# In the gate and up stage of a decoder layer, the product of block B21, which needs no sum, moves ahead to third place

## The chip, the cores and the metric

The kernel runs on one core of a Trainium2 chip. The metric is the device time of one execution in microseconds. The engines are TensorE (PE in the rows, PEld for its weight loads), VectorE (DVE), ScalarE (ACT), GpSimd (POOL, used here almost only to issue DMAs) and SyncE (SP, which issues the weight loads).

## What is computed

One layer of a hybrid decoder over 256 tokens of width 2048, in fp32: three attention branches, gated and merged, an output projection `w_out`, and then a SwiGLU sub-layer of inner width 5632. The change lies in the last of these:

```python
def swiglu(h, w_gate, w_up, w_down):
    return (jax.nn.silu(h @ w_gate) * (h @ w_up)) @ w_down
...
        h = rms_norm(x, norm_ffn_g[l])
        x = x + swiglu(h, w_ffn_gate[l], w_ffn_up[l], w_ffn_down[l])
    return rms_norm(x, final_norm_g)
```

## The kernel before, in words

**fp32 by two halves.** Each fp32 operand is split in two parts that TensorE can multiply: a rounded high part (ACT, line 806 for a gate or up weight) and the rest, the low part (DVE, line 811). A product is three matmuls for each 128 rows: high by high, low activation by high weight, high activation by low weight (`highs_first`, lines 783 to 794). With four slices of 128 rows a weight piece of 512 rows by 512 columns makes twelve matmuls of 128x512 for one PSUM bank.

**A gate and up pair.** `ffn_job(j)` (line 597), for j = 0 to 10, computes 512 columns of both gate and up for the 256 tokens. Of the four pieces of 512 rows, rows 0 and 1 go through a product of 2x2 blocks that has seven multiplications instead of eight (Strassen's scheme in Winograd's form); rows 2 and 3 are multiplied plainly. The blocks are B11 (up, rows 0), B12 (gate, rows 0), B21 (up, rows 1), B22 (gate, rows 1). An `m_unit` is one of the seven multiplications: twelve matmuls into one bank, with sums of activation blocks that were made once ("sp", `combine`, line 494). A `p_unit` is one plain piece for both token halves: twelve matmuls into each of two banks. Four banks are used under the names b6, b5, b8 and b1. The order before (lines 689 to 699) is

1. B11 into b6, copied out by ACT as m1 (`keep`, line 663)
2. B22 into b5
3. B11+B12 into b8, copied out as m5: the "first sum". DVE adds B12 into B11 ahead of its high part (line 612); behind its low part POOL issues a DMA that adds B22 from memory into the piece B12 (line 622, `accum_op`)
4. piece 2 of gate ("2,1") into b5, then b8
5. the "second sum", B11+B12+B22, into b6, copied out as u2, with another DVE add before and a DMA that adds B21 into B11 behind
6. piece 3 of gate ("3,1") into b5, then b8
7. the piece B12 with what was added, into b6, copied out as u3; after it `gate` on DVE and ACT
8. B21 into b1
9. piece 2 of up ("2,0") into b1, then b6
10. the piece B11 with all that was added, into b6
11. piece 3 of up ("3,0") into b1, then b6; after it `up` (lines 678 to 684), three DVE operations that free b6 and b1. 

Then f is transposed by TensorE, copied by ACT ("ft", line 577) and stored by a DMA, as side work of the next pair.

**Weight pieces** of 1 MB come by DMAs on SP's queue in the order of the loop at line 606. At most six raw pieces of this stage are live (`RAWS`, `pump`, line 764); each release of one lets in the next load. Raw pieces, high and low parts and two activation quads share 17 buffers of 1 MB.

**The order of issue** is fixed when the program is built, and each engine takes its instructions in that order. The main loop goes through the units:

```python
    for u, (need, later, stage, _, emit) in enumerate(units):
        prepare_units(u + 4 if stage == "mix" else u + 6)
        advance(1)
        todo, deferred[:] = deferred[:], []
        emit(ready.popleft())
        held -= need + later
        for f in todo:
            f()
```

`prepare_units` (line 934) works under a budget of nine parts for this stage. In steady state one step u issues: the add, if any, and the high part of unit u+4; the low part of unit u+3 with the release or the accumulating DMA behind it; one step of the side work (`advance`); the matmuls of unit u and its copy; then what was deferred. Where the stage begins, the step of the last `w_out` unit issues the low part of the first gate and up unit and the add and high part of the third; the step of the first unit issues the low parts of the second, third and fourth units and the high parts of the fourth and fifth.

**Side work at the start of the stage.** `evac_out(3)` (line 515) ends the mixer: DVE sums x2's last quarter (line 519), and its side steps follow in the first steps of the first pair: two empty ones, then eight transposes by TensorE with line 541 on ACT and line 542 on DVE for the four pieces of the quarter (in the step of the third unit), then ACT's row sums (line 485) and DVE's reciprocal root (in the step of the fourth).

Of the kernel before, what the change touches and what calls it, by code (L numbers as in the profile page):

```python
# [51 lines left out]
def trunk(ctx, tc, xT, x, gmix, gffn, w_in, b_gate, lq1, lk1, lq2, lk2, subln, w_branch, w_out,  # L52
# [12 lines left out]
    def slot(shape, name, dt=F32):  # L65
        return slots.tile(shape, dt, tag="slot", name=name)
# [92 lines left out]
    def quad(key):  # L159
        while key not in quads:  # L160
            assert side, key
            advance(1)
        return quads[key]
# [404 lines left out]
    def f_out(j, f):  # L568

        yield  # L570
        ps = [tps() for _ in range(2)]
        for t in range(2):
            transposes(ps[t], [f[:, t, i * P:(i + 1) * P] for i in range(4)])
        yield
        ft = slot([P, 4, S], "ft")
        for t in range(2):
            nc.scalar.activation(ft[:, :, t * P:(t + 1) * P], ps[t].rearrange("p (a b) -> p a b", a=4), AF.Copy)
        nc.gpsimd.dma_start(f_t[j], ft)
        yield
# [3 lines left out]
    def f_load(q):  # L583
        if q < NCF:
            f_in[q] = slot([P, 4, S], "fin")
            nc.gpsimd.dma_start(f_in[q], f_t[q])
# [10 lines left out]
    def ffn_job(j):  # L597

        B = {(k, n): (j, k, n) for k in range(4) for n in range(2)}
        B11, B12, B21, B22 = B[0, 0], B[0, 1], B[1, 0], B[1, 1]
        aps = {(j, k, n): (w_fu, w_fg)[n][j, k] for k in range(4) for n in range(2)}
        for key in (B11, B22, B12, B[2, 1], B[3, 1], B21, B[2, 0], B[3, 0]):
            want(key, aps[key], "ffn")
        bank = {}
        v = {}

        def add(dst, src):
            nc.vector.tensor_tensor(raw[dst], raw[dst], raw[src], OP.add)  # L612

        def m_unit(op, key, name, adds=(), drop=(), after=None, then=None):
            def prep():
                for d, s in adds:
                    add(d, s)
                h = high(raw[key])
                yield
                l = low(raw[key], h)  # L620
                if then:
                    nc.gpsimd.dma_start(raw[then[0]], aps[then[1]], accum_op=OP.add)
                release(*drop)
                yield h, l

            def emit(w):
                first = name not in bank
                if first:
                    bank[name] = accp.tile([P, 512], F32, tag="acc", name="acc")
                sh, sl = quad(("s", 0))[op]  # L630
                highs_first([(bank[name], sh, sl, first)], w)
                if after:
                    after()
            units.append((1, 1, "ffn", prep, emit))

        def p_unit(k, n, after=None):
            def prep():
                r = raw[B[k, n]]
                h = high(r)
                yield  # L640
                l = low(r, h)
                release(B[k, n])
                yield h, l

            def emit(w):
                qh, ql = quad(("h2", k))
                for t, name in enumerate((("b1", "b6"), ("b5", "b8"))[n]):
                    first = name not in bank
                    if first:
                        bank[name] = accp.tile([P, 512], F32, tag="acc", name="acc")  # L650
                    ts = slice(t * P, (t + 1) * P)
                    highs_first([(bank[name], qh[:, :, ts], ql[:, :, ts], first)], w)
                if after:
                    after()
            units.append((1, 1, "ffn", prep, emit))

        def keep(name, b):
            def f():
                if name == "m1":
                    v["m"] = slot([P, 2, 512], "m")  # L660
                    v["u"] = slot([P, 2, 512], "u")
                v[name] = v["m" if name[0] == "m" else "u"][:, int(name in ("m5", "u3"))]
                nc.scalar.activation(v[name], bank[b], AF.Copy)  # L663
                if name == "u2":
                    deferred.append(lambda: nc.vector.tensor_tensor(v["m5"], v["m5"], v["u2"], OP.subtract))
                if name == "u3":
                    deferred.append(gate)
            return f

        def gate():  # L670
            quad("rs2")
            s = v["s"] = slot([P, 2, 512], "sg")
            nc.vector.tensor_tensor(s[:, 0], bank["b5"], v["m5"], OP.add)
            nc.vector.tensor_tensor(s[:, 1], bank["b8"], v["u3"], OP.subtract)
            for t in range(2):
                nc.scalar.activation(s[:, t], s[:, t], AF.Silu, scale=rs2[:, t:t + 1])

        def up():

            s = v["s"]  # L680
            nc.vector.tensor_tensor(s[:, 1], bank["b6"], s[:, 1], OP.mult)
            nc.vector.tensor_tensor(v["m1"], bank["b1"], v["m1"], OP.add)
            nc.vector.tensor_tensor(s[:, 0], v["m1"], s[:, 0], OP.mult)
            side.append(f_out(j, s))

        def last():
            deferred.append(up)

        m_unit(0, B11, "b6", after=keep("m1", "b6"))
        m_unit(2, B22, "b5")  # L690
        m_unit(4, B11, "b8", adds=[(B11, B12)], after=keep("m5", "b8"), then=(B12, B22))
        p_unit(2, 1)
        m_unit(5, B11, "b6", adds=[(B11, B22)], drop=[B22], after=keep("u2", "b6"), then=(B11, B21))
        p_unit(3, 1)
        m_unit(6, B12, "b6", drop=[B12], after=keep("u3", "b6"))
        m_unit(1, B21, "b1", drop=[B21])
        p_unit(2, 0, after=(lambda: (f_load(0), f_load(1))) if j == NCF - 1 else None)
        m_unit(3, B11, "b6", drop=[B11])
        p_unit(3, 0, after=last)
# [61 lines left out]
    def want(key, ap, stage):  # L761
        wanted.append((key, ap, stage))
# [15 lines left out]
    def release(*keys):  # L778
        for k in keys:
            del raw[k]  # L780
        pump()

    def highs_first(todo, w):


        wh, wl = w
        for acc, ah, al, start in todo:
            for k in range(4):
                first = start and k == 0
                nc.tensor.matmul(acc, ah[:, k], wh[:, k], start=first, stop=False, skip_group_check=not start)  # L790
                nc.tensor.matmul(acc, al[:, k], wh[:, k], start=False, stop=False, skip_group_check=not start)  # L791
        for acc, ah, al, start in todo:
            for k in range(4):
                nc.tensor.matmul(acc, ah[:, k], wl[:, k], start=False, stop=k == 3, skip_group_check=not start)  # L794
# [9 lines left out]
    def high(r):  # L804
        h = big([P, 4, 512], "wh", F32R)
        nc.scalar.activation(h, r, AF.Copy)  # L806
        return h

    def low(r, h):
        l = big([P, 4, 512], "wl", F32R)  # L810
        nc.vector.tensor_tensor(l, r, h.bitcast(F32), OP.subtract)  # L811
        return l
# [72 lines left out]
    for j in range(NCF):  # L885
        ffn_job(j)
# [135 lines left out]
```

## Time and profile before

| | |
|---|---|
| median of 3 runs | 1666.36 us (1666.3 to 1666.77) |
| profiled execution | 1665.84 us, span 1663.7 us, mean granted clock 0.997 |
| PE, DVE, ACT busy in the span | 99%, 64%, 50% |
| chain that ended last | PE 97%, DVE 1%, DMA 1% |
| DMA | 352.65 MB moved, 212 GB/s in the mean |

The span runs from the first to the last instruction on the core. The share of an engine is its busy time over the span; matmuls overlap at their ends, so a busy PE is not one at its peak. The chain that ended last is followed back from the last instruction, at each step to what released it. Times in the rows are in microseconds from the span's start. In a timeline a bracket at the end of a row gives the idle time of the engine before it and what ended it.

### The profile page before, as it was taken

To read this page: it belongs to the slowest core of one execution; us is meant where nothing else is said; L and a number is where in the kernel's file an instruction comes from. 1 tells how busy PE (TensorE), PEld (TensorE's weight loads), DVE (VectorE), ACT (ScalarE), POOL (GpSimd) and SP (SyncE) were. 2 spreads that over 40 slices of the span, in tenths; PEclk is the share of its full clock that TensorE was granted. 3 is DMA by queue.
4 is the path that set the end of the run, shared out by engine and by line. 5 is a ranking of instruction groups with operands and counts; after the bars stand their busy time and mean duration, and the time that the engine had idled before them with its cause. 6 is when DMAs were issued, how large, how long until landed. Compare 5 with 4: busy or idle time off the path is not lost.

```text
span 1663.7 us, 18735 instructions
## 1 busy us (share of the span) xinstructions
PE 1645.7 (99%) x7512; PEld 1357.3 (82%) x7512; DVE 1065.9 (64%) x1077; ACT 824.1 (50%) x950; POOL 59.9 (4%) x87
## 2 busy tenths in 40 slices
PE   9999999999999999999999989999999999999997
PEld 6878788888888888888888878888888888888886
DVE  6675765555565556555565788777777776655463
ACT  7364554444444444444534465555555556444352
POOL 2100000000000000000000000000000001000000
PEclk9999999999999999999999999999999999999999
DMA  8544444444555555556675678888888888655561
GB/s 335 182 169 161 166 155 166 163 162 166 176 174 208 187 205 200 193 202 217 230 254 179 207 208 263 264 265 266 265 266 265 266 265 307 236 201 181 199 244 60
DMA packets 53656, 352.65 MB, mean 212 GB/s; under 512 B 6256, under 2 KB 6528, under 8 KB 13760
## 3 DMA queue, kind: packets, MB, share of 16 engines
q1 hardware_dynamic: 44640, 309.35, 51.4%
q0 software_dynamic: 8208, 41.04, 10.5%
q8 instruction: 59, 0.97, 0.2%
q10 hardware_dynamic: 720, 1.06, 0.2%
q14 instruction: 29, 0.24, 0.0%
HBM read 343.56 MB, written 7.86 MB: 211 GB/s over the span
## 4 chain that ended last, share of the span: by engine, by line
PE 97%; DVE 1%; DMA 1%; ACT 0%; issue 0%; SPq 0%; ACTq 0%; DVEq 0%
PE acc L800 22%; PE acc L802 22%; PE acc L801 22%; PE acc L790 9%; PE acc L791 9%; PE acc L794 9%; PE tps L206 2%; PE sps L245 1%; DVE wl L811 1%; DMA raw<-w_in_t 1%; PE sps L258 0%; PE sps L259 0%; PE sps L257 0%; PE sps L297 0%; PE sps L298 0%
## 5 line engine op out<-in xcount | busy, mean ns | idle before, releaser
L821 DVE TENSOR_TENSOR wboth<-raw,wboth 128x1024 fp32r<-128x1024 f32 (+1 forms) x410 | 500.7, 1235 | 316.3 <-ACT wboth L820 316.0
L820 ACT ACTIVATE wboth<-raw 128x1024 fp32r<-128x1024 f32 (+1 forms) x410 | 423.5, 1052 | 346.4 <-PE acc L802 284.5
L800 PE MATMUL acc<-wboth,hq 128*128 128x512 f32 x1472 | 586.3, 398 | 0.8 <-ACT wboth L820 0.8
L801 PE MATMUL acc<-wboth,hq 128*128 128x512 f32 x1472 | 573.4, 390 | 1.3 <-DVE wboth L821 1.3
L802 PE MATMUL acc<-wboth,hq 128*128 128x512 f32 x1472 | 574.4, 390 | 0.0
L811 DVE TENSOR_TENSOR wl<-raw,wh 128x2048 fp32r<-128x2048 f32 x121 | 275.9, 2289 | 81.2 <-PE acc L794 42.8
L802 PEld LDWEIGHTS acc<-wboth,hq 128*128 128x128 f32 x1472 | 276.3, 188 | 59.4
L800 PEld LDWEIGHTS acc<-wboth,hq 128*128 128x128 f32 x1472 | 276.5, 188 | 58.8 <-issue 2.7
L801 PEld LDWEIGHTS acc<-wboth,hq 128*128 128x128 f32 x1472 | 276.8, 188 | 57.6 <-DVE wboth L821 2.7
L806 ACT ACTIVATE wh<-raw 128x2048 fp32r<-128x2048 f32 x121 | 228.9, 1911 | 102.0 <-DVE raw L612 49.5
L790 PE MATMUL acc<-wh,hq 128*128 128x512 f32 x352 | 138.1, 392 | 5.2 <-ACT m L663 5.2
L791 PE MATMUL acc<-wh,hq 128*128 128x512 f32 x352 | 137.7, 391 | 0.0
L790 PE MATMUL acc<-wh,sp 128*128 128x512 f32 x308 | 120.8, 392 | 0.0
L791 PE MATMUL acc<-wh,sp 128*128 128x512 f32 x308 | 119.9, 389 | 0.0
L794 PE MATMUL acc<-wl,hq 128*128 128x512 f32 x352 | 94.1, 389 | 0.0
L790 PEld LDWEIGHTS acc<-wh,hq 128*128 128x128 f32 x352 | 66.6, 189 | 19.4 <-ACT m L663 5.6
L794 PE MATMUL acc<-wl,sp 128*128 128x512 f32 x308 | 82.4, 389 | 0.0
L791 PEld LDWEIGHTS acc<-wh,hq 128*128 128x128 f32 x352 | 66.7, 189 | 13.8
L794 PEld LDWEIGHTS acc<-wl,hq 128*128 128x128 f32 x352 | 66.1, 188 | 13.8
L794 PEld LDWEIGHTS acc<-wl,sp 128*128 128x128 f32 x308 | 57.8, 188 | 12.0
L791 PEld LDWEIGHTS acc<-wh,sp 128*128 128x128 f32 x308 | 57.9, 188 | 11.6
L790 PEld LDWEIGHTS acc<-wh,sp 128*128 128x128 f32 x308 | 57.9, 188 | 11.6
(193 smaller groups left out, 1044.5 us busy)
## 6 DMA issues: line engine op xcount, KB each, us to landing
raw<-w_in_t SPq DMA_DIRECT2D x116, 1024.0 KB, 4.9
raw<-w_fu_t SPq DMA_DIRECT2D x44, 1024.0 KB, 4.9
raw<-w_fg_t SPq DMA_DIRECT2D x44, 1024.0 KB, 6.6
raw<-w_fd_t SPq DMA_DIRECT2D x44, 1024.0 KB, 4.9
raw<-w_branch_t SPq DMA_DIRECT2D x24, 1024.0 KB, 4.9
raw<-w_out_t SPq DMA_DIRECT2D x16, 1024.0 KB, 4.9
raw<-w_fg_t POOLq DMA_DIRECT2D x11, 1024.0 KB, 7.9
raw<-w_fu_t POOLq DMA_DIRECT2D x11, 1024.0 KB, 8.8
```

Source lines behind the costliest of these rows:

```text
L206: nc.tensor.transpose(dst[:, i * P:(i + 1) * P], s, ident)
L245: nc.tensor.matmul(ps[:, a:b], qt[lo:hi, h, t * P:(t + 1) * P], kt[lo:hi, h, 0:b - a], start=True, stop=True)
L790: nc.tensor.matmul(acc, ah[:, k], wh[:, k], start=first, stop=False, skip_group_check=not start)
L791: nc.tensor.matmul(acc, al[:, k], wh[:, k], start=False, stop=False, skip_group_check=not start)
L794: nc.tensor.matmul(acc, ah[:, k], wl[:, k], start=False, stop=k == 3, skip_group_check=not start)
L800: nc.tensor.matmul(acc, ah[:, k], wh[:, k], start=start and k == 0, stop=False)
L801: nc.tensor.matmul(acc, ah[:, k], wl[:, k], start=False, stop=False)
L802: nc.tensor.matmul(acc, al[:, k], wh[:, k], start=False, stop=stop and k == n - 1)
L806: nc.scalar.activation(h, r, AF.Copy)
L811: nc.vector.tensor_tensor(l, r, h.bitcast(F32), OP.subtract)
L820: nc.scalar.activation(h[:, sl], r[:, sl], AF.Copy)
L821: nc.vector.tensor_tensor(l[:, sl], r[:, sl], h[:, sl].bitcast(F32), OP.subtract)
```

## The change

The unit of B21 becomes the third, behind that of B22 and ahead of the first sum, and the loads follow: B21's piece third, B12's fourth, then the rest in their order. The operations are the same in kind and number.

```diff
@@ -603,7 +603,7 @@
-        for key in (B11, B22, B12, B[2, 1], B[3, 1], B21, B[2, 0], B[3, 0]):
+        for key in (B11, B22, B21, B12, B[2, 1], B[3, 1], B[2, 0], B[3, 0]):
             want(key, aps[key], "ffn")
@@ -688,12 +688,12 @@
         m_unit(0, B11, "b6", after=keep("m1", "b6"))
         m_unit(2, B22, "b5")
+        m_unit(1, B21, "b1", drop=[B21])
         m_unit(4, B11, "b8", adds=[(B11, B12)], after=keep("m5", "b8"), then=(B12, B22))
         p_unit(2, 1)
         m_unit(5, B11, "b6", adds=[(B11, B22)], drop=[B22], after=keep("u2", "b6"), then=(B11, B21))
         p_unit(3, 1)
         m_unit(6, B12, "b6", drop=[B12], after=keep("u3", "b6"))
-        m_unit(1, B21, "b1", drop=[B21])
         p_unit(2, 0, after=(lambda: (f_load(0), f_load(1))) if j == NCF - 1 else None)
         m_unit(3, B11, "b6", drop=[B11])
         p_unit(3, 0, after=last)
```

## Rows read from the trace of the kernel before

**Rows 1.** The page's first part: busy time, share of the span, instructions of each engine.
```profile
PE 1645.7 (99%) x7512; PEld 1357.3 (82%) x7512; DVE 1065.9 (64%) x1077; ACT 824.1 (50%) x950; POOL 59.9 (4%) x87
```

**Rows 2.** Stretches: length, then busy time by engine, granted clock, DMA share, GB/s.
```profile
core 0: us, PE busy (x) PEld busy (x) DVE busy (x) ACT busy (x) POOL busy (x), PEclk, DMA share, GB/s
950.00:965.00 15.00, 9.83 (x49) 7.90 (x47) 13.88 (x11) 8.30 (x10) 0.88 (x1) 0.99 0.83 258
...
965.00:966.00 1.00, 1.00 (x3) 0.81 (x4) 1.00 (x1) 1.00 (x1) 0.00 (x0) 0.50 1.03 213
...
1045.70:1087.40 41.70, 41.70 (x190) 34.63 (x189) 33.23 (x20) 25.02 (x20) 2.31 (x4) 1.00 0.83 265
```

**Rows 3.** Waits from 936 to 985: us in total, times, the longest.
```profile
PE acc L790 <- ACT m L663: 5.2, 1, 5.2
```

**Rows 4.** TensorE's matmuls in order of time, 936 to 985: start, duration, what.
```profile
947.81 0.39 PE L790 MATMUL acc<-wh,sp 128*128 128x512 f32 x1
...
950.53 0.39 PE L790 MATMUL acc<-wh,sp 128*128 128x512 f32 x1
...
964.92 0.80 PE L790 MATMUL acc<-wh,hq 128*128 128x512 f32 x1 [5.17 <-ACT m L663]
...
969.21 0.39 PE L790 MATMUL acc<-wh,sp 128*128 128x512 f32 x1
```

**Rows 5.** ACT in order of time, 936 to 985.
```profile
963.91 0.47 ACT L541 ACTIVATE hq<-tps,gf 128x256 fp32r<-128x256 f32 x1 [0.58 <-DVE hq L542]
964.28 0.59 ACT L663 ACTIVATE m<-acc 128x512 f32<-128x512 f32 x1
964.76 1.91 ACT L806 ACTIVATE wh<-raw 128x2048 fp32r<-128x2048 f32 x1
966.56 0.60 ACT L485 ACTIVATE sps<-x 128x512 f32<-128x512 f32 x1
...
967.69 0.20 ACT L485 ACTIVATION_READ_ACCUMULATOR sps<-x 128x1 f32 x1
```

**Rows 6.** DVE in order of time, 936 to 985.
```profile
940.72 2.29 DVE L612 TENSOR_TENSOR raw<-raw 128x2048 f32<-128x2048 f32 x1
...
948.62 4.49 DVE L811 TENSOR_TENSOR wl<-raw,wh 128x2048 fp32r<-128x2048 f32 x2
953.14 2.29 DVE L612 TENSOR_TENSOR raw<-raw 128x2048 f32<-128x2048 f32 x1
955.35 6.71 DVE L811 TENSOR_TENSOR wl<-raw,wh 128x2048 fp32r<-128x2048 f32 x3
961.98 0.48 DVE L542 SCALAR_TENSOR_TENSOR hq<-tps,gf,hq 128x256 fp32r<-128x256 f32 x1
```

**Rows 7.** POOL: accumulating DMAs as issued, first pair and a later one.
```profile
943.67 0.92 POOL L622 DMA_DIRECT2D raw<-w_fg_t  x1 [78.97 <-DVE raw L612]
...
1086.53 0.88 POOL L622 DMA_DIRECT2D raw<-w_fu_t  x1 [12.90 <-DVE wl L811]
```

**Rows 8.** Line 622, the 22 accumulating DMAs: us from issue to landing.
```profile
DMA to landing us min/median/max: 7.7/8.4/10.2
```

**Rows 9.** SP's queue, 915 to 930: loads as issued.
```profile
918.55 7.13 SPq L775 DMA_DIRECT2D raw<-w_fg_t  x2
```

**Rows 10.** DVE in order of time, around the start of a later pair.
```profile
1077.43 2.29 DVE L612 TENSOR_TENSOR raw<-raw 128x2048 f32<-128x2048 f32 x1
...
1082.02 0.68 DVE L681 TENSOR_TENSOR sg<-acc,sg 128x512 f32<-128x512 f32 x1
...
1083.95 4.48 DVE L811 TENSOR_TENSOR wl<-raw,wh 128x2048 fp32r<-128x2048 f32 x2
```

**Rows 11.** ACT in order of time, the same later pair.
```profile
1079.84 1.92 ACT L806 ACTIVATE wh<-raw 128x2048 fp32r<-128x2048 f32 x1 [3.79 <-DVE raw L612]
1083.19 0.60 ACT L663 ACTIVATE m<-acc 128x512 f32<-128x512 f32 x1 [1.44 <-PE acc L794]
...
1089.53 0.60 ACT L663 ACTIVATE m<-acc 128x512 f32<-128x512 f32 x1 [2.13 <-PE acc L794]
...
1091.83 1.07 ACT L577 ACTIVATE ft<-tps 128x512 f32<-128x512 f32 x2
```

## The prediction

> **What bounds the kernel now.** I read the engines' line first: TensorE is busy for 1645.7 of 1663.7 us [rows 1]. Then the table of stretches: a gate and up pair in mid-run has TensorE busy for 41.70 of 41.70 us, while 950 to 965 has 9.83 of 15.00, and right behind it the granted clock is 0.50, the lower level (1.2 of 2.4 GHz) [rows 2]. So the ten later pairs stand at TensorE's own pace, and nothing can be won in them; only the first pair has a hole. The waits of that stretch name it: one wait of 5.2 us, a matmul behind ACT's line 663 [rows 3]. In the matmuls in order of time a unit of twelve takes 2.72 us (947.81 to 950.53); the second bank of the 2,1 unit, b8, starts at 964.92 after 5.17 us idle, and its twelve take 4.29 us (to 969.21), 1.57 more than 2.72 [rows 4]: the price of the lower clock. Of the 18.0 us in which TensorE is idle, the change can reach these 5.17, and the 1.57 beside them.
>
> Why so late? ACT's copy of bank b8 (line 663, the m5 copy) runs at 964.28 only, right behind the last scaling of x2's quarter 3 (line 541, 963.91) [rows 5]. Lines 541 and 542 go in step, and DVE's first line 542 starts at 961.98, behind two low parts (from 948.62), an add and three low parts without a hole [rows 6]. So DVE's order sets the end of the hole: six big operations in 13.36 us, 2.23 each. One more, the add of B12 into B11, had run at 940.72, in time that DVE had free [rows 6].
>
> **The change, part by part.** No operation is added or removed; units, and all that hangs on them, change places. A step of the loop issues in this order: add and high part four units ahead, low part three ahead, one side step, the unit's matmuls, its copy, deferred work.
>
> (a) First pair. The B21 unit is third, the first sum unit fourth. Its add is asked for one step later, behind x2's last sum, and so loses the free place at 940.72. DVE's order from 948.62 becomes: low B22, add, low B21, low first sum, second add, low 2,1, low second sum, then line 542. That is seven big operations instead of six (the add and low B21 come in, low 3,1 falls behind line 542): 948.62 + 7 x 2.23 = 964.2 instead of 961.98 [rows 6]. ACT is through with line 541 2.30 us after (961.98 to 964.28 before) [rows 5, 6]: 966.5. But the copy now stands one step later, behind what that step's preparation and side step give ACT: the high part of the B12 unit, 1.80 us (964.76 to 966.56), and the row sums, 1.23 (from 966.56; the last piece at 967.69 holds ACT some 0.1) [rows 5]. So it starts at about 969.6; 0.64 later (964.28 to 964.92) b8's part of the 2,1 unit can go [rows 4, 5]: 970.2. TensorE has by then done one unit more, for which before would stand at 964.92 + 2.72 = 967.64. **Loss 2.6 us.** A shorter wait for the 2,1 unit's low part lies inside this hole.
>
> (b) The clock. The hole grows from 5.17 to some 7.8 us (5.3 us more of waiting against 2.72 more of work). No row shows the clock after such a hole: no loss at all (gain 1.57), or twice the one seen (loss 1.57 more). I take the nearest row, the same loss [rows 4]: change 0, ends -1.6 and +1.6.
>
> (c) The transfers in the first pair. The DMA that adds B22 to B12 waits for the first add: its issue at 943.67 came 0.66 after the add of 940.72 (2.29 long) [rows 6, 7]. Here: add to 953.1, issue 953.8, landing at most 10.2 us on [rows 8]: 964.0, before ACT gets to that high part at 966.5. Cost 0, hidden under line 541; without that cover each microsecond late would be one lost. The fourth load, now B12's, is one of two issued between 918.55 and 926 [rows 9], for an add at 951. SP's queue keeps the number of its loads; each released piece lets one in. With B21 released third, the load of 2,0 is let in six units ahead of its use instead of five, and no lead falls below six. Cost 0. Bank b1 is held from early in the pair, and four banks suffice: "up" frees two from 1082.02 on [rows 10], in time for the third and fourth unit. Cost 0.
>
> (d) The m5 copy in a later pair; what is lost here counts ten times. Take the pair whose first unit ends at 1083.2 (its m1 copy) [rows 11]. The third unit ends at about 1089.5 (the m5 copy of before) [rows 11]; the sum unit is now next, to 1092.2, and bank b8 is wanted 2.72 later, at 1094.9. The low part of the first sum takes a buffer that the 3,0 unit frees at its end, 1083.2 - 2.72 = 1080.5. Behind it on DVE stand the three operations of "up" (1082.02 to 1083.95, 1.93) [rows 10], then the second add: 1080.5 + 2.2 + 1.9 = 1084.6. The high part of the second sum starts 2.41 later (1077.43 to 1079.84) [rows 10, 11]: 1087.0. Three high parts of 1.80 and two ft copies (1.07) [rows 5, 11], then the m5 copy: 1093.5 to 1094.1. The slack is 0.8 us; before, the copy came as soon as its unit ended. Behind it on ACT are only high parts with units of time to spare. Cost 0; the upper end, if this chain is longer than worked out by 1.3 us, about one ft pair more, is 10 x 0.5 = 5 us.
>
> (e) The second accumulating DMA (B21 into B11) waits for the low part of the second sum. Before it was issued at 1086.53, 0.3 after that low part (1083.95 + 2.24) [rows 7, 10]. Now the low part ends at 1084.6 + 2.4 + 2 x 2.24 = 1091.5, the issue is at about 1091.9, 5.4 later. The last B11 unit's high part waits for the transfer on ACT; behind it stands the u2 copy, on which bank b6 depends from 1105.8 on (1092.2 + 5.44 for 2,1 + 2.72 for the second sum + 5.44 for 3,1). With the longest landing, 10.2 [rows 8]: 1102.1 + 1.8 + 0.6 = 1104.5. Slack 1.3. Cost 0; the upper end is rival A.
>
> (f) The last pair feeds the down stage as before: its last three units keep their places. Cost 0.
>
> **Sum.** 2.6 us. The profiled execution took 1665.84 us (span 1663.7 and 2.1 around it), 0.5 below the median 1666.36; by its own time the sum gives 1668.4, by the median 1669.0. I forecast 1669.0, up 0.16%. A measurement of this kernel tells apart about 0.2%, 3.3 us, so this is most likely "same". With (b)'s ends: 1667.4 to 1670.6.
>
> **The rivals.** *A, slower: the accumulating transfer lands late in every later pair.* It now runs among more of the pair's loads. The 22 transfers took 7.7 to 10.2 us [rows 8], so company cost one of them up to 2.5. If worse company doubles that, 12.7: landing 1104.6, copy done 1107.0, b6 late by 1.2, ten times, plus 2.6: 1681. It decides from a landing of 11.5 us on. Against it: the same transfers already run beside loads (DMA share 0.83 over the pair [rows 2]) and none took more than 10.2. Chance 0.08.
> By the Trainium skill, "DMA: Bandwidth & Descriptors", section "Queues, rings and completion order", each DMA engine takes packets in turn from the queues that have work, so that the loads of another queue stretch this transfer for as long as they last; the spread of 7.7 to 10.2 agrees with a stretch, and no row shows one as long as rival A needs.
>
> *B, slower: the slack of (d) is gone* and the m5 copy is late by 0.5 us in ten pairs: 1669.0 + 5 = 1674. For it: 0.8 us over a chain of ten operations is little. Against: operations of one kind agree within some hundredths in the rows. Chance 0.05.
>
> *C, faster: the hole closes.* If the B21 unit covered the wait, 5.17 + 1.57 = 6.7 us would go: 1659.6. For that the m5 copy would have to run at about 961.5, so ACT would have to take it ahead of what was issued earlier. For it: one unit more of work stands ahead of the copy's reader. Against: before, the copy ran right behind line 541 though its unit had ended by 957 (964.92 - 5.17 - 2.72) [rows 4, 5]; the queues are served in order. Chance 0.05.
>
> *D, the change does not do what it says*: B21's piece would come too late for a third unit. But the third load was issued before the two at 918.55 [rows 9], and its high part is due at about 940. Chance 0.01, the time about that of the forecast.
>
> **How the numbers follow.** Forecast 0.81, A 0.08, B 0.05, C 0.05, D 0.01. Within the forecast the clock moves 2.6 by up to 1.6 either way, the rest of (a) by some tenths; about a third of it lies above +3.3, none below -3.3. Slower by over 0.2%: 0.27 + 0.08 + 0.05 = 0.40; faster 0.05; within 0.55. The range 1667.0 to 1674.0 takes in the forecast with its clock ends, and B; A and C stay out.
>
> **What would show it.** Right: one wait of 7 to 8 us behind line 663 before b8 of the first 2,1 unit, ending near 970; the first line 542 of x2's quarter 3 at 964; later pairs of 41.7 us with no idle TensorE; high part of B12, row sums, m5 copy in this order on ACT. Wrong: a wait behind line 663 in each later pair (behind m5: B; behind u2, with landings over 11.5: A), or TensorE going on before 967 (C). If only the clock after the hole differs, (b) was mis-sized.

## The result, and the profile after

The changed kernel takes 1678.05 us in the median against 1666.33 before in the same session: a ratio of 1.0074 (95% interval 1.0061 to 1.0087), 11.7 us slower. The forecast was 1669.0 in a range that ended at 1674.0; rival A, which the text had at 1681 with a chance of 0.08, is what happened. The profiled execution has a span of 1675.4 us, 11.7 over the one of before.

The waits say where, as in [rows 3]. All waits of TensorE's matmuls and weight loads behind line 663 in the changed kernel, over the whole span, and what ACT waited for (us in total, times, longest):

```profile
PE acc L790 <- ACT m L663: 6.8, 1, 6.8
PE acc L790 <- ACT u L663: 6.2, 7, 1.3
PEld acc L790 <- ACT u L663: 10.0, 9, 1.7
PEld acc L790 <- ACT m L663: 7.3, 1, 7.3
ACT wh L806 <- DMA raw<-w_fu_t: 78.5, 10, 8.8
```

The single wait behind the m5 copy is still there and longer, 6.8 instead of 5.2 (the row of the weight loads, PEld, covers the same time once more, so the two aren't added). New are nine waits behind a u copy, and before them a wait that the kernel before did not have at all: ACT's high part sits on a DMA ten times, 78.5 us in all. The part of the page on DMA issues names it (1024 KB each, median us from issue to landing):

```profile
raw<-w_fg_t POOLq DMA_DIRECT2D x11, 1024.0 KB, 9.2
raw<-w_fu_t POOLq DMA_DIRECT2D x11, 1024.0 KB, 12.0
```

The second one is the DMA that adds B21 into B11. Its median was 8.8 us before, and no accumulating DMA then took more than 10.2 [rows 8]; now the median is 12.0.

**Where the 11.7 us came from.** The copies of m1 are the mile posts: each stands at the end of a pair's first unit. In the kernel before they lie 41.69 apart. After, ACT in order of time (each pair's m1 copy):

```profile
1002.23 0.60 ACT L663 ACTIVATE m<-acc 128x512 f32<-128x512 f32 x1 [2.17 <-PE acc L794]
...
1044.26 0.60 ACT L663 ACTIVATE m<-acc 128x512 f32<-128x512 f32 x1 [1.71 <-PE acc L794]
...
1087.17 0.60 ACT L663 ACTIVATE m<-acc 128x512 f32<-128x512 f32 x1 [1.70 <-PE acc L794]
...
1129.12 0.60 ACT L663 ACTIVATE m<-acc 128x512 f32<-128x512 f32 x1 [1.70 <-PE acc L794]
...
1172.29 0.60 ACT L663 ACTIVATE m<-acc 128x512 f32<-128x512 f32 x1 [1.70 <-PE acc L794]
...
1386.43 0.60 ACT L663 ACTIVATE m<-acc 128x512 f32<-128x512 f32 x1 [1.71 <-PE acc L794]
```

Nine pairs take 1386.43 - 1002.23 = 384.20 us where nine of 41.69 take 375.2: 9.0 us lost there. Up to 1002.23 the kernel is 2.4 later than before (999.81 then), though the stage was reached 0.4 earlier: 2.8 lost in the first pair. Some 0.3 more comes behind 1386. (The waits behind the u copies give 6.2 by the matmuls and 10.0 by the weight loads, which cover one stretch twice; the mile posts measure the loss itself.)

One pair shows the chain. ACT around 1140 to 1153, and the matmul that waits, in the changed kernel:

```profile
1138.41 1.06 ACT L577 ACTIVATE ft<-tps 128x512 f32<-128x512 f32 x2
1139.36 0.60 ACT L663 ACTIVATE m<-acc 128x512 f32<-128x512 f32 x1
1139.84 1.93 ACT L806 ACTIVATE wh<-raw 128x2048 fp32r<-128x2048 f32 x1
1150.42 1.92 ACT L806 ACTIVATE wh<-raw 128x2048 fp32r<-128x2048 f32 x1 [8.66 <-DMA raw<-w_fu_t]
1152.24 0.58 ACT L663 ACTIVATE u<-acc 128x512 f32<-128x512 f32 x1
```
```profile
1152.88 0.50 PE L790 MATMUL acc<-wh,sp 128*128 128x512 f32 x1 [1.14 <-ACT u L663]
```

ACT stands still for 8.66 us until the DMA has landed, makes the last B11 unit's high part, and only then copies u2; TensorE, which wants bank b6 for the B12 unit, has waited 1.14 us. The engine named by TensorE's wait is ACT, but what ended last is the DMA, and ACT's own row says so.

Pair by pair the loss follows the landing with a slope of one. The landings of the nine pairs between the mile posts are 11.7, 12.5, 11.6, 12.8, 12.7, 11.9, 12.0, 12.9 and 12.7; the pairs take 42.03, 42.91, 41.95, 43.17, 43.12, 42.26, 42.35, 43.34 and 43.07. Each is 41.69 plus what the landing has above some 11.3. In the first pair the DMA lands after 10.6, in the last after 8.8, and neither has a wait behind a u copy.

**Why it lands late.** The DMA's window from issue to landing, in one pair before and one after; packets, MB and share of the 16 engines by queue (q0 is POOL's, q1 is SP's). Before, 1086.53 to 1095.30:

```profile
q0 software_dynamic: 144, 1.05, 65.3%
q1 hardware_dynamic: 141, 1.02, 28.2%
```

After, 1095.64 to 1107.21:

```profile
q1 hardware_dynamic: 311, 2.29, 53.8%
q0 software_dynamic: 169, 1.15, 47.0%
```

POOL's queue gets 0.653 x 8.77 = 5.7 us of all engines in one and 0.470 x 11.57 = 5.4 in the other: about the same work. But beside it SP's loads took 2.5 us before and 6.2 after, with the engines full (the shares add up to 101%). Five microseconds later in the pair the DMA meets more than twice the loads. That isn't only because a longer window holds more: in the first 8.0 us behind the issue SP's queue has 0.68 MB before (1086.53 to 1094.53) and 1.56 after (1095.64 to 1103.64):

```profile
q1 hardware_dynamic: 99, 0.68, 20.8%
```
```profile
q1 hardware_dynamic: 222, 1.56, 55.8%
```

### The profile page after: what moved, and what is told of

Read it like the earlier page. It is cut to its first block, busy times and chain, and to the rows that moved or that the text cites. A ratio compares the mean times of both kernels' runs of the same rounds, so it can differ in the third digit from the quotient of the medians.

```text
span 1675.4 us, 18715 instructions
## 1 busy us (share of the span) xinstructions
PE 1648.7 (98%) x7512; PEld 1356.4 (81%) x7512; DVE 1061.5 (63%) x1077; ACT 822.1 (49%) x950; POOL 59.7 (4%) x87
## 3 DMA queue, kind: packets, MB, share of 16 engines
q0 software_dynamic: 8208, 41.04, 10.2%
## 4 chain that ended last, share of the span: by engine, by line
PE 83%; issue 8%; DMA 6%; DVE 1%; ACT 1%; SPq 0%; POOL 0%; ACTq 0%; POOLq 0%; DVEq 0%
PE acc L800 22%; PE acc L802 22%; PE acc L801 22%; DMA raw<-w_fu_t 6%; PE acc L790 4%; PE acc L791 4%; PE acc L794 4%; PE tps L206 2%; PE sps L245 1%; DVE raw L612 1%; DMA raw<-w_in_t 1%; ACT u L663 0%; DVE wl L811 0%; PE sps L258 0%; PE sps L259 0%
## 5 line engine op out<-in xcount | busy, mean ns | idle before, releaser
L811 DVE TENSOR_TENSOR wl<-raw,wh 128x2048 fp32r<-128x2048 f32 x121 | 274.2, 2288 | 97.1 <-ACT wh L806 53.8
L806 ACT ACTIVATE wh<-raw 128x2048 fp32r<-128x2048 f32 x121 | 228.2, 1913 | 168.8 <-DMA raw<-w_fu_t 78.5
L794 PEld LDWEIGHTS acc<-wl,sp 128*128 128x128 f32 x308 | 57.8, 188 | 12.1
```

## The experiments

Theory L: the second accumulating DMA lands late, ACT waits, and the u2 copy behind that wait holds TensorE; the first pair's loss is separate. Its part W: the landing is late because of the weight loads beside it. Rivals: the new order as such (O), a loss carried on from the first pair (C, not the C of the prediction), the store on the same queue (S).

**The u2 copy on DVE**

```diff
-                nc.scalar.activation(v[name], bank[b], AF.Copy)
+                if name == "u2":
+                    nc.vector.tensor_copy(v[name], bank[b])
+                else:
+                    nc.scalar.activation(v[name], bank[b], AF.Copy)
```

> The changed kernel with the u2 copy on DVE instead of ACT, so that it no longer stands behind the high part that waits for the second accumulating DMA. Theory L (late landing): the waits of TensorE behind the u2 copy in the later pairs go, pairs of 41.7 us again, only the first pair's loss is left: 1668.5 to 1669.5. Rival O (the new order of loads or units itself makes the pairs longer): still 1676 to 1679. The landing of the DMA itself stays near 12 us under L.

1670.56 us, ratio to before 1.0021 (1.0012 to 1.0030). Of the 11.7 us 7.9 are gone with one copy moved, though the DMA lands even later (median 13.1) and ACT still waits for it, 86.1 us in ten times. O falls as the cause of the larger part. The time is 1.1 above the range expected. This kernel's trace has the rest: five of its nine later pairs are still over 41.69, by 0.03 to 0.76 us and 1.55 in all. The u3 copy, still on ACT, is now the one behind the waiting high part:

```profile
PEld acc L793 <- ACT u L666: 1.9, 4, 0.9
```

**Only pair 0, and only the later pairs, in the new order**

```diff
-        for key in (B11, B22, B12, B[2, 1], B[3, 1], B21, B[2, 0], B[3, 0]):
+        early = j == 0
+        for key in ((B11, B22, B21, B12, B[2, 1], B[3, 1], B[2, 0], B[3, 0]) if early else
+                    (B11, B22, B12, B[2, 1], B[3, 1], B21, B[2, 0], B[3, 0])):
...
+        if early:
+            m_unit(1, B21, "b1", drop=[B21])
...
-        m_unit(1, B21, "b1", drop=[B21])
+        if not early:
+            m_unit(1, B21, "b1", drop=[B21])
```

The second kernel has `early = j > 0` in place of `early = j == 0`.

> The new order of units and loads in pair 0 alone. Theory L with the first pair's hole counted apart: about 2.8 us over before, 1669.1. Rival C (the loss starts in the first pair and is carried from pair to pair): most of the 11.7, 1675 or more.

1669.02 us, ratio 1.0014 (1.0005 to 1.0023): 2.3 us.

> The new order in pairs 1 to 10, pair 0 as before. Theory L: nine or ten pairs with some 1.0 us each, 8.9 us over before: 1675.2. Rival C: near before, 1666 to 1669.

1676.53 us, ratio 1.0056 (1.0043 to 1.0068): 9.8 us. The two add up to 12.1, the whole change to 11.7. The parts are independent, and C falls: with pair 0 as before the loss of the later pairs is all there.

**Only the order of the loads**

```diff
-        for key in (B11, B22, B12, B[2, 1], B[3, 1], B21, B[2, 0], B[3, 0]):
+        for key in (B11, B22, B21, B12, B[2, 1], B[3, 1], B[2, 0], B[3, 0]):
```

> The kernel before with only the order of the loads changed (the piece B21 third, B12 fourth); units as before. Theory L: no change, 1665.5 to 1667.5, and the second accumulating DMA lands within 10.5 us of its issue. Rival O (it is the order of the loads): 1670 or more.

1666.91 us, ratio 0.9999 (0.9990 to 1.0008): no difference. No trace shows this kernel's landings at this pace, so that part of the expectation stays open. With the units as before, the order in which the pieces come costs nothing; the new order of the units does.

**The last B11 unit behind the 3,0 unit**

```diff
-        m_unit(3, B11, "b6", drop=[B11])
-        p_unit(3, 0, after=last)
+        p_unit(3, 0)
+        m_unit(3, B11, "b6", drop=[B11], after=last)
```

> The changed kernel with the last B11 unit behind the 3,0 unit, so that its high part is issued one step later, behind the u2 copy. Theory L: the waits for the u2 copy go in all pairs, 1668.5 to 1670 (the landing itself may stay at 12). Rival O: 1676 or more.

1669.14 us, ratio 1.0014 (1.0005 to 1.0023), the time of the kernel with only pair 0 changed. The landing stays late, 12.2 in the median; ACT's waits for it shrink to 26.3 us, no wait behind the u2 copy is left, and every later pair takes 41.69 us in the new order of units, which ends O. With the order of two units swapped, the reader of the DMA is issued behind the copy, and the late landing costs nothing. Of the matmuls' waits behind line 663 only the first pair's, behind m5, is left:

```profile
PE acc L790 <- ACT m L663: 6.8, 1, 6.8
```

**Loads held back beside the DMA**

```diff
-    def release(*keys):
+    def release(*keys, hold=False):
         for k in keys:
             del raw[k]
-        pump()
+        if not hold:
+            pump()
...
-                release(*drop)
+                release(*drop, hold=key == B12 or B22 in drop and op == 5)
...
-                release(B[k, n])
+                release(B[k, n], hold=(k, n) == (3, 1))
```

> The changed kernel; the three releases that follow the second sum (of B22, 3,1 and B12) let in no load, the release of 2,0 lets in all four. So fewer weight loads are under way beside the second accumulating DMA, which is issued as late as in the changed kernel. Theory W (the loads beside it stretch the landing to 12 us): landing 8 to 9.5, the waits behind the u2 copy gone, 1668.5 to 1669.5 (the first pair's loss stays). If the later issue alone is enough for the waits, whatever the landing: 1674 to 1678. A price on the other side would be a late load for the next pair: new waits for pieces at its start.

1670.41 us, ratio 1.0022 (1.0012 to 1.0032). The landing falls to 8.0 us in the median. In one pair's 8.0 us behind the issue, 1055.05 to 1063.05 (this one lands after 7.8), SP's queue has almost nothing:

```profile
q0 software_dynamic: 222, 1.37, 82.3%
q1 hardware_dynamic: 15, 0.08, 2.4%
```

The pairs from the third on are back at 41.69 us. The DMA is issued 7.1 us behind the pair's m1 copy (1055.05 and 1047.95), not quite as late as in the changed kernel (8.5), but 3.8 later than before (1086.53 and 1083.19, 3.3). The 1.4 that it comes earlier would give back most of the loss by itself, so it is the landing and not the time that decides: W holds, without the loads the DMA lands as fast late in the pair as at its old place. The time is 1.4 above that of the kernel with pair 0 alone changed; the second pair takes 42.98 here, 1.3 over the others. TensorE's one wait in it is of f's transposes behind `up`, and no wait for a load is among those around it; why `up` is late there stays open:

```profile
PE tps L206 <- DVE sg L683: 0.8, 1, 0.8
```

**The store of f's transposes on ACT's queue**

```diff
-        nc.gpsimd.dma_start(f_t[j], ft)
+        nc.scalar.dma_start(f_t[j], ft)
```

> The changed kernel with the store of f's transposes issued on ACT's queue instead of POOL's. Theory S (the 12 us come from the store that is issued on the same queue 2.2 us after the accumulating DMA): median landing of the second accumulating DMA falls to 10 or less and the time to 1669 to 1671. Theory W (they come from the weight loads that are under way beside it): landing stays at 11.5 or more, time 1676 to 1679.

1692.1 us, ratio 1.0144 (1.0127 to 1.0162): 14 us worse than the changed kernel, and S falls the hard way. The landing went up to 13.7 in the median, 1.7 more than 12.0. TensorE's waits in this kernel, and a row of its page's part on DMA issues:

```profile
PE acc L790 <- ACT u L663: 18.8, 9, 2.7
PEld acc L790 <- ACT u L663: 22.6, 9, 3.1
```
```profile
raw<-w_fu_t POOLq DMA_DIRECT2D x11, 1024.0 KB, 13.7
```

The waits behind the u copies are there as in the changed kernel, and 12.6 us longer in all (18.8 against 6.2; the weight loads' row, 22.6 against 10.0, says the same once more). On POOL's queue the store stood behind the DMA; on a queue of its own all of it runs beside the DMA: in one window from issue to landing, 1057.36 to 1071.58, it is the third row:

```profile
q1 hardware_dynamic: 378, 2.78, 54.6%
q0 software_dynamic: 144, 1.05, 36.6%
q10 hardware_dynamic: 143, 0.52, 9.3%
```

Pair by pair L's slope of one holds for five of the nine later pairs: one of 44.60 us is 2.9 over 41.69, with a landing 2.9 over 11.3. The other four are 1.5 to 2.9 us longer than their landings make them (the longest takes 47.59, 5.9 over, with a landing of 14.3). In these four, and in no other, the granted clock falls to 0.50 at the wait behind the u copy. Two of them and, between them, one of the five (length, then busy time by engine, granted clock, DMA share, GB/s):

```profile
1028.80:1032.00 3.20, 3.20 (x9) 2.52 (x8) 3.20 (x3) 2.65 (x2) 0.00 (x0) 0.50 0.43 84
1074.00:1078.00 4.00, 3.89 (x17) 3.24 (x18) 4.00 (x3) 4.00 (x4) 0.00 (x0) 1.00 0.30 63
1162.00:1168.60 6.60, 6.11 (x14) 4.79 (x15) 5.61 (x4) 4.62 (x5) 0.00 (x0) 0.50 0.50 180
```

So a late landing can cost twice: of the 29.5 us that the nine pairs lose some 22 go with the landings, and some 7.5 with the lower clock.

**The accumulating DMA later, in the kernel before** (a miss, then a surprise)

```diff
-        def p_unit(k, n, after=None):
+        def p_unit(k, n, after=None, then=None):
...
+                if then:
+                    nc.gpsimd.dma_start(raw[then[0]], aps[then[1]], accum_op=OP.add)
...
-        m_unit(5, B11, "b6", adds=[(B11, B22)], drop=[B22], after=keep("u2", "b6"), then=(B11, B21))
-        p_unit(3, 1)
+        m_unit(5, B11, "b6", adds=[(B11, B22)], drop=[B22], after=keep("u2", "b6"))
+        p_unit(3, 1, then=(B11, B21))
```

> The kernel before, with the DMA that adds B21 into B11 issued one step later, behind the low part of the 3,1 unit; order of units and loads as before. Its reader is far off, so the time should stay: 1665.5 to 1667.5. What it measures is the landing: if it is the later place in the pair that costs (more loads and the store beside it), median 11 or more where before has 9; if it is the new order of units, 10 or less.

1666.39 us, ratio 0.9998 (0.9989 to 1.0007), landing 8.8. It tells nothing on the place: the first issue stands at 960.2 as it did before (960.14). POOL has nothing else in its queue there, so the DMA goes when its data are ready, wherever the program has it. To move it, it has to stand behind something that POOL waits for:

```diff
-        m_unit(5, B11, "b6", adds=[(B11, B22)], drop=[B22], after=keep("u2", "b6"), then=(B11, B21))
+        m_unit(5, B11, "b6", adds=[(B11, B22)], drop=[B22], after=keep("u2", "b6"))
...
-        m_unit(1, B21, "b1", drop=[B21])
+        m_unit(1, B21, "b1", drop=[B21], then=(B11, B21))
```

> The kernel before, with the DMA that adds B21 into B11 issued behind the low part of the B21 unit and so, on POOL, behind the store of f's transposes: some 7 us later in the pair, about where the changed kernel has it. Units and loads as before; there the u2 copy is issued ahead of the high part that waits for the DMA. Theory L: the time stays, 1665.5 to 1667.5, although ACT now waits for the landing in each pair: a late landing costs only where a copy stands behind it. If a late landing costs by itself: 1672 or more. Landing under W: over 9, as there are more loads under way at that place.

1695.48 us, ratio 1.0170 (1.0150 to 1.0190). The landing is 12.6 in the median with the units and loads in the order of before: it is the place in the pair that makes it late, and in one window of 12.75 us SP's queue has 2.29 MB and half of the engines. A smaller part may be the store of f's transposes, which is now issued just ahead on POOL's queue: that queue's packets take 0.508 x 12.75 = 6.5 us of all engines here, 0.8 more than before. The two were not separated. But the expectation that the time stays was wrong. The u2 copy is ahead of the waiting high part here, yet others stand behind it. ACT stands for 8.2 us, then DVE, whose low part needs that high part, for 7.8, and what DVE owes comes late: the longest total of TensorE's waits is now the f transposes behind line 683 of "up". TensorE's waits and DVE in one pair:

```profile
PE tps L206 <- DVE sg L683: 18.2, 9, 2.5
```
```profile
1069.59 4.49 DVE L811 TENSOR_TENSOR wl<-raw,wh 128x2048 fp32r<-128x2048 f32 x2 [7.82 <-ACT wh L806]
```

So L was too narrow in naming the u2 copy alone: a stop in a queue served in order delays all behind it, on the next engine too.

**The first pair's hole, in the kernel before**

```diff
-                for _ in range(2 if c == 3 else 1):
+                for _ in range(3 if c == 3 else 1):
                     yield
```

> The kernel before, with the side work of x2's last quarter one step later, so that the m5 copy of the first pair stands ahead of line 541 on ACT. If the hole of the first pair is ACT's queue order alone: the copy runs near 961.5, TensorE goes on near 962, 2.5 to 4 us won: 1662.5 to 1664. If the 3,1 unit then waits for x2's last quarter instead: 1665 to 1667.

1661.57 us, ratio 0.9972 (0.9962 to 0.9982): 5.2 us faster than the kernel before, and the fastest of all here. ACT and TensorE around the hole:

```profile
957.67 3.71 ACT L806 ACTIVATE wh<-raw 128x2048 fp32r<-128x2048 f32 x2
961.27 0.59 ACT L663 ACTIVATE m<-acc 128x512 f32<-128x512 f32 x1
```
```profile
961.92 0.50 PE L790 MATMUL acc<-wh,hq 128*128 128x512 f32 x1 [2.32 <-ACT m L663]
```

The copy runs at 961.27, ahead of line 541, and the hole is 2.32 us. The granted clock over 955 to 965 is 1.00, so the price of the lower clock went too. 5.17 - 2.32 + 1.57 = 4.4; the spans of the two traced executions differ by 4.2 (1659.5 and 1663.7), so the trace shows no other gain; the rest of the 5.2 between the medians stays open.

## Why the prediction was wrong, point by point

**(e) failed.** It put the landing at 10.2 at most, the longest of the 22 of before, and so found 1.3 us of slack. The issue was placed right: 8.7 us behind the m1 copy was worked out, 8.5 measured (1095.64 and 1087.17). The slack was even right: a landing beyond some 11.5 was named as the point from which it decides, and the pairs begin to lose at 11.3. What was wrong is the use of [rows 8]: those landings belong to the place the DMA had, with 1.0 MB of loads on its way in the pair shown. The change moves it to a place with 2.3 MB. The trace of before had the means to see it: the issue was worked out for 1091.9, and SP's queue there, in the kernel before, from 1091.9 to 1099.9, has three times the 0.68 MB that it has in the 8.0 us behind the old issue:

```profile
q1 hardware_dynamic: 275, 2.10, 65.4%
```

The share of 0.83 [rows 2], a mean over the whole pair, was taken to say that the DMA already had such company.

**Rival A** had the mechanism, the place and nearly the time (1681 for 1678): landing 12.7 against 12.0 measured, 1.2 us late in each pair against 1.0. That the time came so near is in part luck: the 12.7 was a doubling and not worked out from the loads, and it was charged to ten pairs where nine lose. Its chance of 0.08 was too low for an argument that rested on the same row and on the mean share. By the Trainium skill, "DMA: Bandwidth & Descriptors", section "Queues, rings and completion order", the engines take turns between the queues that have work. The runs agree at three points: 7.8 us with 0.08 MB of another queue's loads on the way, 8.8 with 1.0, 11.6 with 2.3; and a third queue made it 13.7 in the median. The page's rule deserved more than a sentence beside the rival.

**(a) held, to a tenth.** Seven big operations on DVE, then line 542, the high part of B12, the row sums and the copy, in that order. After, from 948.22 (0.4 earlier than before):

```profile
963.75 0.48 DVE L542 SCALAR_TENSOR_TENSOR hq<-tps,gf,hq 128x256 fp32r<-128x256 f32 x1
```
```profile
966.05 1.90 ACT L806 ACTIVATE wh<-raw 128x2048 fp32r<-128x2048 f32 x1
967.86 0.59 ACT L485 ACTIVATE sps<-x 128x512 f32<-128x512 f32 x1
...
969.08 0.58 ACT L663 ACTIVATE m<-acc 128x512 f32<-128x512 f32 x1
```
```profile
969.71 0.79 PE L790 MATMUL acc<-wh,hq 128*128 128x512 f32 x1 [6.82 <-ACT m L663]
...
974.37 0.60 PE L235 MATMUL sps<-ident,rs 128*128 128x128 f32 x4
```

With the 0.4 the second bank starts at 970.1 for 970.2 worked out. **(b)** was within its ends: b8's twelve took 4.66 us (969.71 to 974.37) for 4.29 before, 0.4 more. Together 2.8, and 2.3 in the median of the kernel with pair 0 alone changed.

**(c)** had its zero right and its landing wrong: the first pair's DMA that adds B22 to B12 was issued at 953.36 (953.8 worked out) and took 12.1 us, where 10.2 at most had been used here too. It was there at 965.5, only 0.6 before ACT came to that high part (966.05). For the order of the loads the zero held (ratio 0.9999). **(d)** held: no wait behind the m5 copy in a later pair, and the copy comes 10.24 us behind m1 (1097.41 and 1087.17) for 10.3 to 10.9 worked out; so rival B fell. **Rival C** fell: the hole grew. **D** fell: the third unit ran without a wait. **(f)** was not tested by itself; some 0.3 us are lost behind the last mile post.

## What to carry to other kernels

A measured landing is the landing of one place in time: before a transfer is moved, lay its new issue beside the other queues' transfers and count their bytes. In these runs an instruction that waited for a transfer stopped its whole engine (ACT for 8.66 us here), so put it behind the short copies that another engine waits for; here a swap of two units, or one copy on another engine, gave back most of the loss. And look at the hole that is there: moving a side step by one, which cost no operation, won more than any order of the pairs could, since the pairs already ran at TensorE's pace.

## What was not expected of the hardware

The packets of an accumulating DMA of 1 MB took 5.7 us of the 16 engines (0.653 x 8.77), where SP's loads took 2.4 per MB in that window and 2.7 in the one after (53.8% of 11.57 us for 2.29 MB): about twice as long for the same bytes. Moving a 512 KB store from the DMA's queue to an idle third one made the DMA land 1.7 us later, not earlier. And the length of a hole alone doesn't tell what the clock does behind it. Behind the first pair's 5.2 us the granted clock was 0.50 for about 3.4 us, behind 6.8 us for about 7 in the changed kernel and for about 10 in two others with the same hole (the u2 copy on DVE, the last B11 unit behind 3,0), and behind 2.3 it stayed at 1.00 (the side step later). But with the store on ACT's queue it fell at a wait of 2.1 in one pair and stayed up at one of 2.6 in another.
